# The mixer's projection: who makes the low halves of the weights

## The chip, the cores and the metric

The kernel runs on one core of a Trainium2 chip. The core has a matrix engine (TensorE, "PE" in the profile, with "PEld" for its weight loads), VectorE ("DVE"), ScalarE ("ACT"), GpSimd ("POOL") and SyncE ("SP"), which issues most of the DMAs. Each engine works through its own queue of instructions in order; between engines there are semaphores. The metric is the device time of one execution in microseconds (us); the median of three runs is used.

## The reference

One layer of a streaming encoder on a sequence of 1024 rows of width 1024, all in float32:

```python
h = sublayer(h, 0, swiglu_1, 0.5)          # feed-forward block, 1024 -> 2816 -> 1024
h = sublayer(h, 1, token_mixer, 1.0)       # the mixer
h = sublayer(h, 2, swiglu_2, 0.5)          # feed-forward block

def token_mixer(u, w_in, ...):
    proj = u @ w_in                        # 1024 x 5120
    qa, ka, va, qd, kd, vd, ga, gd = jnp.split(proj, IN_SPLITS, axis=-1)
    ya = stick_breaking_attention(heads(qa, 8), heads(ka, 8), heads(va, 8))
    yd = differential_attention(qd1, qd2, kd1, kd2, heads(vd, 4), lam)
    yd = rms_norm(yd, subln) * (1.0 - lambda_init)
    merged = jax.nn.sigmoid(ga) * (ya @ w_branch_sb) + jax.nn.sigmoid(gd) * (yd @ w_branch_da)
    return merged @ w_out
```

Each sublayer has a normalisation and a modulation before it and a normalisation and a gate behind it. The mixer's first product is the projection `proj = u @ w_in`; its columns are the queries, keys and values of two kinds of attention and the two gates.

## The kernel before, in words

**Products in two halves.** TensorE multiplies a rounded form of float32 ("fp32r"). To keep the precision, each operand is cut in a high half (the value rounded) and a low half (the value less its high half), and a product is made of three matmuls: high by high, high by low, low by high. For a weight tile the helper `split` (lines 135 to 143) does this: SyncE loads 128 x 1024 numbers into a tile `raw` (line 138, two buffers), ScalarE casts it to `wsH` (line 141), and VectorE subtracts, `wsL = raw - wsH` (line 142). `wsH` and `wsL` have four buffers each. `split` takes the engine of the subtraction as an argument, VectorE by default.

**The mixer.** Its first part projects and attends, its second merges. In the first part the projection is cut in jobs (class `Job`, line 791). A job owns one or two weight tiles and makes one slice of the projection: `QJob` and `KJob` 128 columns of queries or keys (eight jobs each, one weight tile each), `GateJob` 128 columns of a gate (sixteen, one tile), `VJob` 256 columns of values (four, two tiles). That is 8 + 8 + 16 + 4 x 2 = 40 weight tiles. A job of 128 columns runs 48 matmuls of 512 columns (lines 813, 815, 817), the third of which is the first to read `wsL`.

**Attention, and what fills it.** Eight units follow one another, four of stick-breaking attention (two heads each) and four of differential attention. In a unit, TensorE makes scores (lines 938, 939), ScalarE and VectorE turn them into weights, TensorE transposes them (lines 955, 956), ScalarE and VectorE cut the transposed weights in halves (`tH`, line 960, 963 or 965; `tL`, line 961, 964 or 966), and TensorE multiplies them with the values (line 1021 or 1066). In the stick-breaking units VectorE's part is a scan (line 1010) and a product of two tiles (line 1011) for each row block; in the differential units a scaling (line 1055) and a combination (line 1056). The matmuls of the jobs for the next unit and of the gates are put between those of the attention by `fill` and `advance`: in each call the next few matmuls of the first job in the list are traced, and `advance_` (line 923) calls `load` for the first two jobs of the list, so that a job's tiles are asked for one job ahead.

**What sets the order.** The instructions of each engine are put in order when the program is built, by the Tile framework's planner: it starts from the order in which they are traced and lets each engine take what its own model of times says is ready. Where a buffer is used again, it adds the waits. So an instruction that goes to another engine can also change the order of those around it. GpSimd's queue holds little in the mixer: `KJob` (lines 866, 867) has it copy each half of the keys to the other 64 partitions, 64 instructions of 64 x 512. SyncE's queue holds, in the mixer, the loads of `raw`, the stores of the gates (line 878) and the stores of the attention's results (lines 1027, 1088).

**The first jobs.** The first `QJob`, `KJob` and `VJob` have their tiles loaded while the last product of the first feed-forward block still runs. The second part of the mixer (the merge) calls `split` directly, for `wbs`, `wbd` and `wo`, 32 tiles; the two feed-forward blocks have helpers of their own for their weights (line 226).

Of the kernel before, what the change touches and what calls it, by code (L numbers as in the profile page):

```python
# [770 lines left out]
def mixer(e):  # L771
# [5 lines left out]
    V, ACT, PE, POOL, SP = nc.vector, nc.scalar, nc.tensor, nc.gpsimd, nc.sync  # L777
    split, mm3, wproj, ident = n.split, n.mm3, n.wproj, n.ident
# [7 lines left out]
    with tc.tile_pool(name="mixa", bufs=1, side="left", reuse_waits="tile") as pa, \  # L786
# [4 lines left out]
        class Job:  # L791
# [7 lines left out]

            def load(self):  # L800
                if self.w is None:
                    self.w = [split(s) for s in self.srcs]

            def step(self):
                if self.it is None:
# [342 lines left out]
        for u in range(8):  # L1148
            sb = u < 4
            if u == 4:  # L1150

                with tc.issue_after(last_act[0].ins):
                    load = ACT.add_instruction(mybir.InstLoadActFuncSet(
                        name=nc.get_next_instruction_name(), engine=ACT.engine, act_func_set_id=EXP_LN_TABLE))
                order.enter_context(tc.issue_after(load.ins if hasattr(load, "ins") else load))
# [196 lines left out]
```

## Time and profile before

| | us |
|---|---|
| median of three runs (lowest, highest) | 2268.05 (2264.48, 2269.99) |
| the profiled execution's own time | 2263.8 |
| its span in the profile | 2261.9 |
| granted TensorE clock, mean | 0.988 |
| PE busy | 2169.0 (96%) |
| DVE busy | 1565.4 (69%) |
| ACT busy | 1043.2 (46%) |
| POOL busy | 70.2 (3%) |

How to read the profile: an engine is busy while it executes; a row of a group of instructions gives line, engine, operation, what is written and read, the shape and the count, then busy time and the mean of one in ns, then the idle time of that engine just before them and what ended it. A table by stretches gives the busy time of each engine in a piece of the span, with the number of its instructions in brackets. A timeline has the start, the duration and the instruction, and in square brackets the idle time before it.

### The profile page before, as it was taken

Reading aid. Unit: us, or ns where it says so; the run is one execution under the profiler, and the core shown is the slowest. Engines: PE = TensorE matmul, PEld = TensorE weight load, DVE = VectorE, ACT = ScalarE, POOL = GpSimd, SP = SyncE. Lnnn points to the kernel's source line nnn. Section 1 sums busy time; section 2 is a strip of 40 time slices with the busy share of each in tenths; the row PEclk is TensorE's granted clock in tenths of the full one; section 3 lists DMA queues with packets and bytes.
Section 4 is the critical chain, followed back from the end, with each engine's and each line's share of the span. In section 5 each row is a group of like instructions: output and inputs, shape, how many; then the busy total and the mean of one; then the engine's idle time right before and its main releaser. Section 6 shows DMA issues by size and latency. Waiting matters only on the chain. (4 is left out here: it accounts for less than half of the span.)

```text
span 2261.9 us, 28622 instructions
## 1 busy us (share of the span) xinstructions
PE 2169.0 (96%) x10420; PEld 1792.0 (79%) x10420; DVE 1565.4 (69%) x2612; ACT 1043.2 (46%) x1882; POOL 70.2 (3%) x90
## 2 busy tenths in 40 slices
PE   5999999999999999999999999999999999999998
PEld 3777778878887877878888988788878788887886
DVE  6886877567677687576677577656886666755566
ACT  4633323325466556455545455555743232434454
POOL 1000000000000010011011010000000000000000
PEclk8899999999999999999999999999999999999999
DMA  7284874449787111110211122764475553538676
GB/s 307 79 280 164 300 258 170 147 161 314 250 276 228 60 32 45 38 48 30 62 57 59 45 96 75 236 200 139 149 242 186 177 177 135 186 117 270 210 225 217
DMA packets 137677, 364.38 MB, mean 161 GB/s; under 512 B 16704, under 2 KB 20800, under 8 KB 137536
## 3 DMA queue, kind: packets, MB, share of 16 engines
q1 hardware_dynamic: 135904, 356.79, 46.6%
q0 software_dynamic: 1632, 5.77, 0.7%
q8 instruction: 81, 1.33, 0.2%
q14 instruction: 60, 0.49, 0.1%
HBM read 272.32 MB, written 90.18 MB: 160 GB/s over the span
## 5 line engine op out<-in xcount | busy, mean ns | idle before, releaser
L813 PE MATMUL pps<-uH,wsH 128*128 128x512 f32 x512 | 209.0, 408 | 0.0
L815 PE MATMUL pps<-uL,wsH 128*128 128x512 f32 x512 | 204.5, 399 | 0.0
L817 PE MATMUL pps<-uH,wsL 128*128 128x512 f32 x512 | 203.6, 398 | 0.0
L226 DVE TENSOR_TENSOR tbL<-stg,tbH 128x512 fp32r<-128x512 f32 x154 | 105.9, 690 | 104.8 <-ACT tbH L225 104.3
L225 ACT CAST tbH<-stg 128x512 fp32r<-128x512 f32 x154 | 95.7, 621 | 156.7 <-DMA stg<-d_T 113.1
L298 PE MATMUL bank<-uH,wsH 128*128 128x512 f32 x352 | 142.2, 406 | 6.4 <-DVE uH L180 2.9
L584 PE MATMUL bankA<-tbL,sbH 128*128 128x512 f32 x352 | 138.8, 394 | 6.3 <-DVE tbL L226 6.3
L299 PE MATMUL bank<-uL,wsH 128*128 128x512 f32 x352 | 140.2, 398 | 1.4 <-POOL uL L181 1.3
L300 PE MATMUL bank<-uH,wsL 128*128 128x512 f32 x352 | 138.7, 395 | 0.0
L583 PE MATMUL bankA<-tbH,sbH 128*128 128x512 f32 x352 | 138.4, 395 | 0.1
L585 PE MATMUL bankA<-tbH,sbL 128*128 128x512 f32 x352 | 138.3, 393 | 0.1
L142 DVE TENSOR_TENSOR wsL<-raw,wsH 128x1024 fp32r<-128x1024 f32 x72 | 88.0, 1222 | 69.3 <-ACT wsH L141 68.0
L226 DVE TENSOR_TENSOR sbL<-stg,sbH 128x512 fp32r<-128x512 f32 (+1 forms) x176 | 108.2, 620 | 29.6 <-ACT sbH L225 26.9
L225 ACT CAST wsH<-s 128x1024 fp32r<-128x1024 f32 x88 | 92.0, 1049 | 72.4 <-DVE s L332 54.2
L225 ACT CAST sbH<-stg 128x512 fp32r<-128x512 f32 (+1 forms) x176 | 98.2, 565 | 52.7 <-DMA stg<-hd_A 37.6
L365 ACT COPY q<-bank 128x512 f32<-128x512 f32 x44 | 25.8, 586 | 207.1 <-PE bank L300 207.1
L817 PEld LDWEIGHTS pps<-uH,wsL 128*128 128x128 f32 x512 | 96.8, 189 | 17.4
L226 DVE TENSOR_TENSOR wsL<-s,wsH 128x1024 fp32r<-128x1024 f32 x88 | 107.2, 1219 | 3.5 <-ACT wsH L225 3.5
L813 PEld LDWEIGHTS pps<-uH,wsH 128*128 128x128 f32 x512 | 97.6, 191 | 14.3
L815 PEld LDWEIGHTS pps<-uL,wsH 128*128 128x128 f32 x512 | 97.1, 190 | 14.2
L225 ACT CAST wsH<-raw 128x1024 fp32r<-128x1024 f32 (+1 forms) x88 | 73.2, 834 | 71.5 <-PE bank L299 38.9
L583 PE MATMUL bankB<-tbH,sbH 128*128 128x512 f32 x264 | 102.8, 389 | 0.0
(247 smaller groups left out, 5941.2 us busy)
## 6 DMA issues: line engine op xcount, KB each, us to landing
wada<-in_wada SPq DMA_DIRECT2D x56, 512.0 KB, 5.2
raw<-in_wg SPq DMA_DIRECT2D x50, 512.0 KB, 6.4
raw<-in_wu SPq DMA_DIRECT2D x50, 512.0 KB, 4.5
raw<-in_wd SPq DMA_DIRECT2D x44, 512.0 KB, 4.5
stg<-hd_A SPq DMA_DIRECT2D x88, 256.0 KB, 4.2
stg<-d_S SPq DMA_DIRECT2D x88, 256.0 KB, 3.5
stg<-d_T SPq DMA_DIRECT2D x88, 256.0 KB, 3.8
d_S<-s SPq DMA_DIRECT2D x40, 512.0 KB, 2.7
```

Of the source, the lines that this page charges most:

```text
L142: eng.tensor_sub(l, raw, h.bitcast(F32))
L225: ACT.copy(h, src)
L226: V.tensor_sub(l, src, h.bitcast(F32))
L298: PE.matmul(ps, H[:, ks], bH, start=first and k == 0, stop=False, skip_group_check=not first)
L299: PE.matmul(ps, H[:, ks], bL, start=False, stop=False, skip_group_check=not first)
L300: PE.matmul(ps, L[:, ks], bH, start=False, stop=k == 3, skip_group_check=not first)
L583: PE.matmul(ps, sH[:, ts], tH, start=first, stop=False, skip_group_check=not check)
L584: PE.matmul(ps, sH[:, ts], tL, start=False, stop=False, skip_group_check=not check)
L585: PE.matmul(ps, sL[:, ts], tH, start=False, stop=last, skip_group_check=not check)
L813: PE.matmul(ps, aH, bH, start=i == 0, stop=False)
L815: PE.matmul(ps, aH, bL, start=False, stop=False)
L817: PE.matmul(ps, aL, bH, start=False, stop=i == n - 1)
```

## The change

`Job.load` hands GpSimd to `split`, which uses it for the subtraction. Load, cast and buffers stay as they are, and so do the 32 tiles of the merge, which call `split` without the argument.

```diff
             def load(self):
                 if self.w is None:
-                    self.w = [split(s) for s in self.srcs]
+                    self.w = [split(s, eng=POOL) for s in self.srcs]
```

The helper that is called, unchanged:

```python
    def split(src, pool=None, tag="ws", bufs=4, eng=V):
        raw = wpool.tile([P, D], F32, name="raw", tag="raw", bufs=2)
        SP.dma_start(raw, src)
        h = (pool or wpool).tile([P, D], F32R, name="wsH", tag=tag + "H", bufs=bufs)
        l = (pool or wpool).tile([P, D], F32R, name="wsL", tag=tag + "L", bufs=bufs)
        ACT.copy(h, raw)
        eng.tensor_sub(l, raw, h.bitcast(F32))
        return h, l
```

## The prediction

> **What bounds the kernel now.** I first read the page's busy times, then a table by stretches over the mixer's projection and attention, cut at the change of units: the run-in (644 to 780 us), the four stick-breaking units (780 to 1100) and the four differential units (1100 to 1420).
>
> ```profile
> PE 2169.0 (96%) x10420; PEld 1792.0 (79%) x10420; DVE 1565.4 (69%) x2612; ACT 1043.2 (46%) x1882; POOL 70.2 (3%) x90
> ...
> core 0: us, PE busy (x) PEld busy (x) DVE busy (x) ACT busy (x) POOL busy (x), PEclk, DMA share, GB/s
> 644.00:780.00 136.00, 128.87 (x681) 110.33 (x680) 92.84 (x166) 76.72 (x148) 5.33 (x8) 0.97 0.56 182
> 780.00:1100.00 320.00, 299.48 (x1708) 249.16 (x1707) 232.37 (x322) 177.88 (x399) 29.28 (x32) 0.99 0.13 40
> 1100.00:1420.00 320.00, 317.90 (x1798) 275.45 (x1797) 224.17 (x677) 158.27 (x345) 18.09 (x24) 1.00 0.21 70
> ```
>
> TensorE bounds the whole and each of these stages. Its idle time is all that a change on another engine can win: 136 - 128.87 = 7.1 us in the run-in, 320 - 299.48 = 20.5 us in the stick-breaking units, 320 - 317.90 = 2.1 us in the differential units; 29.7 us in all. The rest of its time is matmuls, whose number stays. So the question is what the 20.5 us wait for. From the waits of TensorE between 780 and 1100 (us in total, times, longest):
>
> ```profile
> PE pav L1021 <- DVE tL L961: 10.8, 7, 3.0
> PE pav L1021 <- ACT tH L965: 3.0, 4, 1.9
> PE trp L956 <- DVE be L1011: 2.1, 3, 1.1
> PE pav L1021 <- DVE tL L966: 1.9, 5, 0.7
> ```
>
> VectorE ends 10.8 + 2.1 + 1.9 = 14.8 us of these waits, each time with work of the attention. Nobody in the mixer's first part waits for the low halves themselves: in the view of line 142 the only waiters are the merge's matmuls (L201).
>
> ```profile
> L142 DVE TENSOR_TENSOR wsL<-raw,wsH x72: 1204/1224/1227, 644.5 to 1571.5; 128x1024 fp32r<-128x1024 f32 x72
> ...
> who waited for it (us, times):
>   PEld ops L201: 0.6, 1
>   PE ops L201: 0.2, 1
> ```
>
> The attention's waits on VectorE look like this (timeline, 802 to 808.5):
>
> ```profile
> 802.41 2.28 DVE L1010 TENSOR_TENSOR_SCAN f<-f 128x1024 f32<-128x1024 f32 x1
> ...
> 803.00 1.05 ACT L141 CAST wsH<-raw 128x1024 fp32r<-128x1024 f32 x1
> ...
> 804.61 0.67 DVE L961 TENSOR_TENSOR tL<-trp,tH 128x512 fp32r<-128x512 f32 x1
> 805.19 1.21 DVE L1011 TENSOR_TENSOR be<-be,f 128x1023 f32<-128x1023 f32 x1
> ...
> 805.33 0.51 PE L1021 MATMUL pav<-tL,v 128*128 128x256 f32 x2 [1.67 <-DVE tL L961]
> ...
> 806.65 1.22 DVE L142 TENSOR_TENSOR wsL<-raw,wsH 128x1024 fp32r<-128x1024 f32 x1
> ...
> 807.79 0.28 DVE L966 TENSOR_TENSOR tL<-trp,tH 128x128 fp32r<-128x128 f32 x1
> ...
> 808.13 0.33 PE L1021 MATMUL pav<-tL,v 128*128 128x128 f32 x1 [0.32 <-DVE tL L966]
> ```
>
> The large gap, 1.67 us, comes from a long scan ahead of `tL`, with no weight work in it; only the small one, 0.32 us, stands behind a `wsL`.
>
> **The change part by part.** *What it takes off VectorE.* Forty subtractions of 1224 ns (the row above; 72 less the merge's 32), 49.0 us. Also the time in which VectorE stands at the head of its queue waiting for the cast. In the stick-breaking units:
>
> ```profile
> L1010 DVE TENSOR_TENSOR_SCAN f<-f 128x128 f32<-128x128 f32 (+3 forms) x64 | 86.8, 1362 | 15.6 <-ACT f L1007 15.1
> L1011 DVE TENSOR_TENSOR be<-be,f 128x127 f32<-128x127 f32 (+3 forms) x64 | 48.1, 757 | 1.1
> ...
> L142 DVE TENSOR_TENSOR wsL<-raw,wsH 128x1024 fp32r<-128x1024 f32 x15 | 18.3, 1223 | 9.1 <-ACT wsH L141 8.1 <-PE trp L956 1.0
> ```
>
> That is 18.3 + 9.1 = 27.4 us given back to VectorE in the stage that has the gaps.
>
> *What it adds on GpSimd.* No row shows this subtraction there. The nearest is the same operation at half the width, at the start of the kernel, and what stood beside it on VectorE:
>
> ```profile
> L181 POOL TENSOR_TENSOR uL<-u,uH x6: 1278/1572/1713, 23.0 to 54.4; 128x512 fp32r<-128x512 f32 x6
> ...
> 20.52 1.23 DVE L226 TENSOR_TENSOR wsL<-raw,wsH 128x1024 fp32r<-128x1024 f32 x1
> ...
> 23.00 1.28 POOL L181 TENSOR_TENSOR uL<-u,uH 128x512 fp32r<-128x512 f32 x1 [21.69 <-DVE uH L180]
> ...
> 23.42 1.94 DVE L226 TENSOR_TENSOR wsL<-raw,wsH 128x1024 fp32r<-128x1024 f32 x1 [0.51 <-ACT wsH L225]
> ```
>
> Twice the width costs no less than 1.28 us and no more than 2 x 1.71 = 3.4 us; I take 2 x 1.28 = 2.5 us (an estimate), as 1.28 us is the undisturbed one of the six. Forty are 100 us, on an engine that is busy 5 + 29 + 18 = 53 us of these 776.
>
> The section on elementwise work in the Trainium skill's GPSIMD Engine Reference gives 4497 ns against 2293 ns for an addition of 2048 columns; by that ratio of 1.96 it would be 2.4 us here, which would change the sums below by a twenty-fifth.
>
> *What the two engines do to each other.* The second quoted VectorE row took 1.94 us where the first took 1.23: GpSimd's subtraction had started at 23.00 and ended at 24.28, and VectorE's, begun at 23.42, ran most of its own length after that. It goes the other way round too (timeline, 1052 to 1059, against the view of the key copies):
>
> ```profile
> L866 POOL CAST kd<-kd x32: 608/612/2413, 741.1 to 1314.8; 64x512 fp32r<-64x512 f32 x32
> ...
> 1053.14 2.29 DVE L1010 TENSOR_TENSOR_SCAN f<-f 128x1024 f32<-128x1024 f32 x1
> 1053.42 2.41 POOL L866 CAST kd<-kd 64x512 fp32r<-64x512 f32 x1 [5.26 <-ACT kd L864]
> 1055.34 0.66 DVE L865 TENSOR_TENSOR kl<-pps,kd 64x512 fp32r<-64x512 f32 x1
> ```
>
> A copy of 0.61 us takes 2.41 us beside a scan. So operations of VectorE with both inputs in SBUF (scans, lines 1011, 142, 226) and GpSimd's take turns, whole instruction by whole instruction. In the stick-breaking units scans and products hold 86.8 + 48.1 = 134.9 of 320 us, 42%. Fifteen subtractions hold 15 x 2.5 = 37.5 us, of which VectorE would want 42%: 15.8 us blocked. Net, VectorE gains 27.4 - 15.8 = 11.6 us on 232.4 us of work, 5.0%. The gaps that it causes, 14.8 us, shrink with it by 0.7 us if they follow its load, and I round this to 1.0 us, for the queue is also freer of waits. From below: a gain of all that VectorE causes, 14.8 us, excluded in practice by the scans in the gaps; from above: 15 holds that each push a chain, priced among the rivals.
>
> The Trainium skill's SBUF — State Buffer says, in its section on the engine side, that VectorE and GpSimd share one pair of ports as an exclusive lock, and that the loser "fully blocks". The trace agrees (1.94 for 1.23, 2.41 for 0.61). Without that rule the sum would give VectorE all 27.4 us, 12% of its load, and a gain of 1.7 us; with it, 0.7.
>
> *The differential units and the run-in.* TensorE is idle for 2.1 us in the first, so there is nothing to win, and what blocks VectorE (lines 1055, 1056) is hidden by a TensorE that has job matmuls to run. In the run-in four subtractions move beside the last feed-forward product, whose 7.1 us of idle TensorE come later, from normalisation. Both 0; cover gone, one gap of a hold, 2.5 us, for each.
>
> *The weights themselves.* They come 1.3 us later, or up to 2.3 us more if a scan holds the lock. TensorE reads most of them tens of us later; the tightest is the first tile of the differential units:
>
> ```profile
> 1099.31 1.22 DVE L142 TENSOR_TENSOR wsL<-raw,wsH 128x1024 fp32r<-128x1024 f32 x1
> ...
> 1102.00 0.60 PE L817 MATMUL pps<-uH,wsL 128*128 128x512 f32 x1
> ```
>
> Begun at 1099.31, it would end at 1101.8 with 2.5 us: 0.2 us in hand. Taken as 0; 3.4 us would cost 0.7.
>
> *The queues.* GpSimd now waits for casts, and the key copies stand behind that; SyncE's loads into `raw` wait for the subtraction of two tiles before, and stores stand behind them.
>
> ```profile
> SPq L138 <- DVE wsL L142: 140.4, 26, 23.2
> ...
> ACT wsH L141 <- DMA raw<-in_win: 3.8, 2, 2.5
> ...
> PEld z L938 <- POOL kl L867: 0.5, 1, 0.5
> ```
>
> SyncE is parked at these loads for 140.4 us already, yet the cast waited for one only twice, 3.8 us: a load freed 1.3 us later is still early. TensorE waited for a key copy once, 0.5 us. Both 0; with the cover gone, one hold of 2.5 us for a copy at the edge of a unit.
>
> *The sum.* The profiled execution took 2263.8 us (2261.9 of span and 1.9 around it); less 1.0 is 2262.8. That execution is 4.25 us below the median of the runs, 2268.05, so the median forecast is 2267 us. A measurement of this kernel tells 0.3%, 6.8 us, from no change.
>
> **The rivals.** *A, faster: the gaps follow VectorE's queue more than its load.* What counts would be how soon `tL` gets a turn, and the planner, with VectorE freer, would put it ahead of scans. Then two thirds of the 14.8 us go: 2268 - 9.9 = 2258 us. For it: 8.1 us of VectorE's standing at the cast; against it: the 1.67 us gap has no `wsL` near it. Chance 0.25.
>
> *B, slower: the lock falls into the scan chains.* In the timeline above the cast ends at 804.05, while the scan runs to 804.69. GpSimd then takes the lock at 804.69 and holds it to 807.19; the product due at 805.19 starts 2.0 us later, and `tL` of line 966 comes, with 1.22 us of `wsL` gone from the queue, 0.8 us later than now; that wait ends last for TensorE. Were that so for all 15, 12 us: 2280 us. It decides from the point at which casts end during a scan more often than between chains; scans alone hold 86.8 of 320 us, 27%, which speaks against it, and for it speaks that the gaps stand just at the long scans, where nothing is in hand. Chance 0.15.
>
> The Trainium skill's Perfetto Trace Analysis, in its section on optimizing, warns that offloading between these two engines "might not help" for their shared port; that is B's mechanism or my forecast, by its size.
>
> *C, slower: lateness on GpSimd reaches TensorE.* Key copies behind a blocked subtraction and the tight tiles: two holds at the starts of units and 3.4 us at the tight tile, 2 x 2.5 + 3.4 = 8.4 us, 2276 us. For it: one queue now carries both; against it: the slack above. Chance 0.10.
>
> **How the numbers follow.** The forecast has 0.50, with its own range of 2261 to 2275 (6.8 us on either side). Faster by over 0.3% is A, 0.25; slower B and C, 0.25. The range takes in A's and B's points with a little of the runs' scatter (2264.48 to 2269.99 before): 2256 to 2282.
>
> **What would show it.** Line 142 should have 32 instructions on VectorE and 40 on GpSimd, of about 2.5 us, longer beside scans; products of line 1011 longer than now by the blocked time, about 16 us in all; VectorE's busy time between 780 and 1100 (which counts the blocked time) near 232 - 18 + 16 = 230 us; TensorE's idle time there near 20 us. TensorE waiting for a `wsL` or a key copy would mean C; longer waits for `tL`, B; idle time near 10 us, A. Wrong altogether would be a TensorE that gains or loses more than 7 us outside the mixer.

## The result

| | before | after |
|---|---|---|
| median of five runs (lowest, highest), us | 2268.05 (2264.48, 2269.99) | 2283.43 (2277.98, 2288.25) |
| profiled execution, its span, us | 2263.8, 2261.9 | 2282.8, 2281.0 |

The change makes the kernel slower: the ratio of the times is 1.0073, with a 95% interval of 1.0057 to 1.0089. The median lies 1.4 us above the upper end of the predicted range.

The first part of the page after, and the views of the moved line and of its neighbours on VectorE. In a view of a line, the three numbers are the shortest, the median and the longest in ns; in a group's row they are the busy time in us and the mean in ns.

```profile
PE 2176.9 (95%) x10420; PEld 1797.9 (79%) x10420; DVE 1555.0 (68%) x2572; ACT 1044.6 (46%) x1882; POOL 164.9 (7%) x130
```

```profile
L142 POOL TENSOR_TENSOR wsL<-raw,wsH 128x1024 fp32r<-128x1024 f32 x40 | 98.4, 2464 | 555.1 <-ACT wsH L141 492.6 <-issue 43.6 <-PE z L939 12.7
```

```profile
L142 POOL TENSOR_TENSOR wsL<-raw,wsH x40: 2362/2402/3345, 644.0 to 1361.7; 128x1024 fp32r<-128x1024 f32 x40
L142 DVE TENSOR_TENSOR wsL<-raw,wsH x32: 1210/1224/1228, 1388.6 to 1588.5; 128x1024 fp32r<-128x1024 f32 x32
```

```profile
L1010 DVE TENSOR_TENSOR_SCAN f<-f 128x128 f32<-128x128 f32 (+3 forms) x64 | 90.5, 1416 | 20.0 <-ACT f L1007 19.5
L1011 DVE TENSOR_TENSOR be<-be,f 128x127 f32<-128x127 f32 (+3 forms) x64 | 58.0, 908 | 1.2
```

```profile
L1011 DVE TENSOR_TENSOR be<-be,f x64: 277/816/2842, 786.7 to 1110.1; 128x127 f32<-128x127 f32 x8, 128x255 f32<-128x255 f32 x8, 128x383 f32<-128x383 f32 x8, 128x511 f32<-128x511 f32 x8
```

Forty subtractions moved and take 2.40 us each on GpSimd in the median; the products of line 1011, which nobody edited, take 58.0 us in place of 48.1, the longest of them 2.84 us; the scans of line 1010 take 90.5 in place of 86.8. Where the time went is read from stages that end at the same work. I cut both executions at the start of the first, the third, the 21st and the last of the 32 jobs of 128 columns. Before, then after:

```profile
727.80:780.20 52.40, 50.22 (x324) 46.25 (x323) 29.05 (x53) 23.84 (x44) 5.33 (x8) 0.97 0.18 61
780.20:1188.20 408.00, 387.45 (x2230) 327.19 (x2229) 290.11 (x489) 218.10 (x486) 34.99 (x40) 0.99 0.15 46
1188.20:1401.20 213.00, 211.40 (x1180) 181.60 (x1179) 155.37 (x492) 106.96 (x240) 12.38 (x16) 1.00 0.20 67
```

```profile
730.90:781.90 51.00, 48.82 (x324) 44.72 (x323) 26.07 (x50) 23.73 (x44) 9.79 (x11) 1.00 0.20 64
781.90:1203.90 422.00, 390.68 (x2229) 328.79 (x2228) 284.02 (x466) 218.25 (x485) 90.55 (x63) 0.98 0.14 44
1203.90:1418.50 214.60, 211.65 (x1179) 181.85 (x1179) 152.08 (x481) 107.43 (x240) 37.47 (x27) 1.00 0.20 67
```

(The columns are the stretch, its length and the busy time of PE, PEld, DVE, ACT and POOL, then the granted clock.) The middle row, which holds the stick-breaking units and the first differential one, has 14.0 of the 19.1 us by which the spans differ. In it TensorE's idle time went from 408.00 - 387.45 = 20.6 us to 422.00 - 390.68 = 31.3 us, while VectorE was busy for 6 us less. So 10.7 us of the row's 14.0 are idle time, and 3.2 us are longer matmuls; of the rest, 1.7 us lie ahead of the row (781.9 - 780.2) and 1.6 and 1.8 us behind it.

TensorE's waits between 780 and 1112 after the change:

```profile
PE pav L1021 <- DVE tL L961: 10.8, 7, 3.0
PE pav L1021 <- ACT tH L965: 5.3, 6, 1.9
PE pav L1021 <- DVE tL L966: 4.0, 5, 2.1
PE trp L956 <- DVE be L1011: 3.5, 4, 1.4
PE trp L955 <- DVE be L1011: 1.3, 1, 1.3
```

The waits that stood there before (`tL` of line 961 behind a scan) are the same 10.8 us in seven. New are those behind line 1011: 3.5 + 1.3 us in place of 2.1, and `tH` of line 965 and `tL` of line 966, which follow it, 9.3 us in place of 4.9. One such place, the same one that the prediction showed for before:

```profile
805.38 2.28 DVE L1010 TENSOR_TENSOR_SCAN f<-f 128x1024 f32<-128x1024 f32 x1
...
806.02 1.05 ACT L141 CAST wsH<-raw 128x1024 fp32r<-128x1024 f32 x1
...
807.14 2.69 POOL L142 TENSOR_TENSOR wsL<-raw,wsH 128x1024 fp32r<-128x1024 f32 x1 [20.73 <-ACT wsH L141]
...
807.58 0.66 DVE L961 TENSOR_TENSOR tL<-trp,tH 128x512 fp32r<-128x512 f32 x1
808.16 2.75 DVE L1011 TENSOR_TENSOR be<-be,f 128x1023 f32<-128x1023 f32 x1
...
810.84 0.41 DVE L964 TENSOR_TENSOR tL<-trp,tH 128x256 fp32r<-128x256 f32 x1
...
811.60 0.33 PE L1021 MATMUL pav<-tH,v 128*128 128x128 f32 x1 [1.53 <-ACT tH L965]
```

GpSimd's subtraction comes in at the end of the scan. The product behind it, 1.21 us before, takes 2.75 us. The `tL` of line 961 between them, one of whose inputs (`trp`) lies in PSUM, keeps its 0.66 us. The `tL` behind the product is late, then `tH`, and TensorE stands for 1.53 us; before, this second gap was 0.32 us. Five of the 64 products stand beside a subtraction of GpSimd in this trace, and each of the five takes 2.74 to 2.84 us.

### The profile page after: what moved, and what is told of

Its sections match the earlier page's. It is cut to its first block, busy times and chain, and to the rows that moved or that the text cites. A ratio compares the mean times of both kernels' runs of the same rounds, so it can differ in the third digit from the quotient of the medians.

```text
span 2281.0 us, 28648 instructions
## 1 busy us (share of the span) xinstructions
PE 2176.9 (95%) x10420; PEld 1797.9 (79%) x10420; DVE 1555.0 (68%) x2572; ACT 1044.6 (46%) x1882; POOL 164.9 (7%) x130
## 4 chain that ended last, share of the span: by engine, by line
PE 59%; DVE 21%; DMA 10%; ACT 5%; issue 3%; SPq 0%; DVEq 0%; ACTq 0%
PE bank L300 8%; PE bank L298 8%; PE bank L299 8%; PE pps L815 4%; PE pps L813 4%; PE pps L817 4%; DMA stg<-d_T 3%; DVE f L1010 3%; DMA stg<-in_wd 2%; DVE wsL L226 2%; PE bankA L583 2%; PE bankA L584 2%; PE bankA L585 2%; DMA wada<-in_wada 1%; DVE be L1011 1%
## 5 line engine op out<-in xcount | busy, mean ns | idle before, releaser
L142 POOL TENSOR_TENSOR wsL<-raw,wsH 128x1024 fp32r<-128x1024 f32 x40 | 98.4, 2464 | 555.1 <-ACT wsH L141 492.6
L1010 DVE TENSOR_TENSOR_SCAN f<-f 128x128 f32<-128x128 f32 (+3 forms) x64 | 90.5, 1416 | 20.0 <-ACT f L1007 19.5
```

The source lines that it names most:

```text
L1010: V.tensor_tensor_scan(fr, fr, fr, 1.0, ALU.mult, ALU.bypass)
```

## The experiments

The theory is the one of the prediction's rival B: VectorE's instructions with two inputs in SBUF and GpSimd's that read SBUF take turns, so each subtraction on GpSimd holds up VectorE's scans and products, and these set the pace of the attention. The rivals are lateness of the weights or of the queues (C), a new order of the instructions from the planner, and, on the other side, that time given back to VectorE has a worth (the forecast and A).

### The same reading, with nothing moved

`split` gets a flag that `Job.load` sets for the 36 tiles that are loaded within the units:

```diff
         eng.tensor_sub(l, raw, h.bitcast(F32))
+        if beside:
+            x = mpool.tile([P, D + 64], BF16, name="scr", tag="junk", bufs=1)
+            POOL.tensor_sub(x[:, :D], raw, h.bitcast(F32))
```

> VectorE keeps all its subtractions (as in the kernel before); beside that GpSimd makes the same difference of raw and wsH once more for the 36 tiles that are loaded within the units, into a scratch tile that nobody reads. Theory (turns at SBUF): GpSimd's 36 holds of about 2.4 us block VectorE's scans and products as in the changed kernel, and nothing is given back: slower than before by at least as much as the change, 15 to 30 us; VectorE's line 1011 rows as long as after the change. Rival (lateness of the weights or of the queues, or the new order of the instructions): nobody waits for this work, so within 5 us of the kernel before.

Measured: 2301.59 us, ratio 1.0141 (1.0109 to 1.0173), about twice the loss of the change. The spare work in this kernel, and what it does to VectorE's own subtractions and to the products (line numbers are shifted by the edit):

```profile
L145 POOL TENSOR_TENSOR scr<-raw,wsH 128x1024 bf16<-128x1024 f32 x36 | 111.3, 3092 | 397.5 <-ACT wsH L141 303.1 <-issue 93.9
```

```profile
L142 DVE TENSOR_TENSOR wsL<-raw,wsH 128x1024 fp32r<-128x1024 f32 x43 | 66.9, 1556 | 30.9 <-ACT wsH L141 30.7
L1015 DVE TENSOR_TENSOR be<-be,f 128x127 f32<-128x127 f32 (+3 forms) x64 | 57.4, 901 | 1.1
```

No engine takes a result from this work, and no weight comes from GpSimd. The products are as long as after the change (57.4 and 58.0 us). By the ratio the loss is 32 us, just above the 15 to 30 of the expectation: the spare subtractions are longer than the moved ones (3092 ns in the mean against 2464), and VectorE's own subtractions, which now stand beside them, take 1556 ns in place of 1224.

Lateness of the weights or of the queues can make little of this loss: in the mixer's first part of this trace TensorE's weight loads wait for a low half once, 0.8 us, and for a key copy once, 2.3 us (0.5 before), and ScalarE's casts wait for `raw` for 5.6 us in all, against 6.2 before. The planner's order can make none of it: in the traces of this kernel and of the kernel before, the instructions of TensorE, VectorE and ScalarE stand in the same order throughout, by operation, tiles and shape.

### The same place and time on GpSimd, with nothing read

```diff
+        if beside:
+            x = mpool.tile([P, D + 64], BF16, name="scr", tag="junk", bufs=1)
+            ACT.copy(x[:, :1], h[:, :1].bitcast(F32))
+            for _ in range(3):
+                POOL.memset(x[:, :D], 0.0)
```

> As the run with GpSimd's spare subtraction, but GpSimd fills the scratch tile with a constant three times instead, behind a one-column copy by ScalarE that ties it to the same place in time; it reads nothing from SBUF. Theory (turns only between instructions that read): VectorE's rows of line 1011 keep their length of before (748 ns median), and the time stays within 5 us of before. If any GpSimd work in these places costs time: 10 us or more slower, as with the subtraction.

Measured: 2271.71 us, ratio 1.0016 (1.0007 to 1.0026).

```profile
L1017 DVE TENSOR_TENSOR be<-be,f 128x127 f32<-128x127 f32 (+3 forms) x64 | 48.3, 760 | 1.1
```

```profile
L147 POOL MEMSET scr<- 128x1024 bf16 x108 | 103.6, 959 | 359.7 <-ACT scr L145 355.8
```

GpSimd is as busy with it as with the moved subtractions after the change (103.6 us against 98.4), in the same places, and the products are as short as before, though 13 of the 64 have a filling beside them. So it is the reading, not GpSimd's being busy. This agrees with the Trainium skill's SBUF — State Buffer, section "Who interferes with whom": an instruction of VectorE with two SBUF inputs contends with one of GpSimd that reads SBUF, and not with one that only writes it. A loss of 3.6 us (1.6 to 5.9, by the ratio) is left, which is clear of zero; 36 small copies of ScalarE are among its possible causes, and it was not taken apart.

### VectorE freed, and nobody loaded

`split` is handed the low half of the first tile, `low`, and leaves its subtraction out once that has been made:

```diff
-        eng.tensor_sub(l, raw, h.bitcast(F32))
+        if low is None or not lows:
+            eng.tensor_sub(l, raw, h.bitcast(F32))
...
-                    self.w = [split(s) for s in self.srcs]
+                    self.w = []
+                    for s in self.srcs:
+                        if low:
+                            self.w.append((split(s, low=low[0])[0], low[0]))
...
```

> Leaves out 39 of the 40 subtractions: all jobs of the projection use the low half of the first tile. So VectorE is freed as by the change and nobody takes the work on. Theory: the gaps come from the scans and the time given back to VectorE is worth little: 0 to 5 us faster than before. Rival A of the prediction (the gaps follow VectorE's queue): 8 to 12 us faster.

Measured: 2268.42 us, ratio 0.9992 (0.9980 to 1.0003): no difference that is clear of zero. The middle stage of this kernel, by the same cuts:

```profile
779.60:1184.20 404.60, 384.47 (x2229) 325.39 (x2229) 265.83 (x466) 218.31 (x485) 33.06 (x40) 1.00 0.15 46
```

VectorE has 290.11 - 265.83 = 24.3 us less to do in it, and TensorE's idle time is 404.60 - 384.47 = 20.1 us, against 20.6 before. In the traces, then, the time given back is worth half a microsecond; by the interval of the times it is worth 4.5 us at most. So rival A's 9.9 us are excluded. The forecast's 1 us is too small for these times to tell, and a version that only takes these subtractions off VectorE has hardly anything to win.

This kernel also settles the new order of the instructions. Apart from the subtractions of weights, its trace has the order of the changed kernel, not of the one before: against the changed kernel 2 of VectorE's other 2364 instructions stand elsewhere, 1 of ScalarE's 1882 and 3 of TensorE's 10420; against the kernel before, 106, 29 and 40 do. With the changed order and nothing on GpSimd, nothing is lost.

### Shorter turns

`split` makes the low half in several pieces on GpSimd, for all 40 tiles:

```diff
-        eng.tensor_sub(l, raw, h.bitcast(F32))
+        for i in range(cuts):
+            c = slice(i * D // cuts, (i + 1) * D // cuts)
+            eng.tensor_sub(l[:, c], raw[:, c], h[:, c].bitcast(F32))
```

> GpSimd makes the low halves as in the change, but each in four subtractions of 256 columns. Theory (turns, whole instruction by whole instruction): a hold is 0.6 to 0.7 us in place of 2.4, VectorE gets its turn after one of them, so the loss falls from 15 us to 0 to 7. Rival (lateness of the weights, GpSimd's queue): GpSimd's work is as long or longer, so the loss stays at 12 us or more.

> As the run with four cuts, with eight subtractions of 128 columns for each tile. Theory (turns): VectorE's waits get shorter still, but each piece has a fixed part and there are twice as many turns: 2 to 7 us slower than before, like four cuts; never faster than before, since freeing VectorE altogether won nothing.

Measured: four pieces 2275.52 us, ratio 1.0025 (1.0009 to 1.0040); eight pieces 2277.46 us, ratio 1.0045 (1.0028 to 1.0063), against 1.0073 with whole tiles. GpSimd's work and the products with four pieces:

```profile
L144 POOL TENSOR_TENSOR wsL<-raw,wsH 128x256 fp32r<-128x256 f32 x160 | 129.6, 843 | 526.0 <-ACT wsH L141 465.5 <-issue 42.9 <-PE z L941 12.4
```

```profile
L144 POOL TENSOR_TENSOR wsL<-raw,wsH x160: 723/744/2191, 645.3 to 1356.0; 128x256 fp32r<-128x256 f32 x160
```

```profile
L1013 DVE TENSOR_TENSOR be<-be,f x64: 280/826/1516, 787.7 to 1104.8; 128x127 f32<-128x127 f32 x8, 128x255 f32<-128x255 f32 x8, 128x383 f32<-128x383 f32 x8, 128x511 f32<-128x511 f32 x8
```

GpSimd works longer (129.6 us against 98.4, a piece 744 ns in the median) and the loss falls to about a third, 5.7 us (2.0 to 9.1): the longest product is 1.52 us in place of 2.84, and the longest before the change was 1.54. VectorE's turn comes after one piece. The order is again that of the changed kernel, with VectorE's and ScalarE's instructions all in the same places. This is what turns of whole instructions give, and what lateness or order does not. Eight pieces lose 10 us (6.4 to 14.3), more than the 2 to 7 expected, though the intervals of four and eight overlap; the reason was not found.

### Which tiles

`Job.load` picks the engine by the unit in which the tile is loaded, for example:

```diff
-                    self.w = [split(s) for s in self.srcs]
+                    self.w = [split(s, eng=POOL if 0 <= unit[0] < 4 else V) for s in self.srcs]
```

> GpSimd makes the low halves of the 16 tiles that are loaded in the four stick-breaking units, VectorE those of the other 24. Theory (holds between scans and products): nearly the whole loss is here, 8 to 14 us slower than before. If the loss went by the number of tiles that GpSimd makes: 16 of 40, 6 us.

> GpSimd makes the low halves of the 20 tiles that are loaded in the four differential units, VectorE those of the other 20. Theory: TensorE had 2 us of idle time there and its queue has other matmuls, so 1 to 4 us slower than before. By the number of tiles: half of the loss, 8 us.

> GpSimd makes the low halves of the first four tiles alone, beside the last product of the first feed-forward block. Theory: no scans there, 0 to 2 us slower than before. If the longer half-clock stretch behind the first feed-forward block (10.2 us after the change, 3.4 before, from about 688) belongs to the change: 3 us.

> GpSimd makes the low halves of the tiles that are loaded in the first differential unit alone (the first six or so of the 20), VectorE all others. In the trace of the run with all four differential units, the first two of these holds fall into the last product of the last stick-breaking unit (2.76 us in place of 1.21), and TensorE's idle time grows there. If that place is most of the loss: 3 to 6 us slower than before. If the loss goes by the number of tiles: 2 to 3 us.

> GpSimd makes the low halves of the tiles that are loaded in the last three differential units alone. If nearly all of the loss of the differential units sits at their start: 0 to 2 us slower than before. If small operations that wait out a hold (line 1045, 2.36 us at most in place of 0.15) cost TensorE time too: 3 to 6 us.

| tiles on GpSimd | median, us | ratio (95%) | by the ratio, us |
|---|---|---|---|
| 16, stick-breaking units | 2277.71 | 1.0039 (1.0026 to 1.0053) | 8.8 (5.9 to 12.0) |
| 20, differential units | 2275.57 | 1.0033 (1.0019 to 1.0048) | 7.5 (4.3 to 10.9) |
| 4, run-in | 2269.86 | 1.0010 (0.9998 to 1.0022) | 2.3 (-0.5 to 5.0) |
| first differential unit alone | 2269.40 | 1.0007 (0.9995 to 1.0019) | 1.6 (-1.1 to 4.3) |
| last three differential units alone | 2271.56 | 1.0013 (1.0000 to 1.0026) | 2.9 (0.0 to 5.9) |

The last column is the ratio less one, times 2268. The first three rows give 18.6 us together, and the change as a whole 16.6 (12.9 to 20.2): the parts add up. A tile of the stick-breaking units costs 0.55 us, one of the differential units 0.38; that of the run-in is not clear of zero. So the stick-breaking units carry about half of the loss, not nearly all of it, and the expectation for the differential units was too low. By the last two rows their loss is 4.5 us, which lies within the interval of the row of all four; 4 to 8 us is as close as these times come. The middle row of the kernel with the stick-breaking units moved, then the middle and the last row of the one with the differential units moved, by the same cuts:

```profile
780.50:1196.70 416.20, 387.59 (x2229) 326.76 (x2229) 286.59 (x475) 218.28 (x486) 67.66 (x54) 0.99 0.14 45
```

```profile
784.10:1195.80 411.70, 388.98 (x2229) 327.84 (x2228) 285.07 (x480) 218.09 (x485) 57.64 (x49) 0.98 0.15 45
1195.80:1410.40 214.60, 211.64 (x1180) 181.79 (x1179) 152.17 (x481) 107.41 (x239) 37.48 (x27) 1.00 0.20 67
```

With the stick-breaking units' tiles moved, TensorE's idle time in the middle row is 28.6 us against 20.6 before. With the differential units' it is 22.7, and 3.0 against 1.6 in the last row: 3.5 us more, at the lower end of what the times allow.

What the trace shows of it is two things. At the seam, the first two subtractions run back to back, and the last product of the last stick-breaking unit stands beside them (timeline of the run with the differential units):

```profile
1100.82 5.67 POOL L142 TENSOR_TENSOR wsL<-raw,wsH 128x1024 fp32r<-128x1024 f32 x2 [38.13 <-issue]
...
1101.49 2.76 DVE L1012 TENSOR_TENSOR be<-be,f 128x1023 f32<-128x1023 f32 x1
...
1104.31 0.47 PE L957 MATMUL trp<-ident,be 128*128 128x128 f32 x1 [1.03 <-DVE be L1012]
```

And within the units small operations wait out a hold. The maximum of two numbers per row, before and after the change:

```profile
L1045 DVE TENSOR_TENSOR mx<-mx x32: 136/152/161, 1151.6 to 1388.3; 128x1 f32<-128x1 f32 x32
```

```profile
L1045 DVE TENSOR_TENSOR mx<-mx x32: 139/154/2358, 1166.4 to 1405.7; 128x1 f32<-128x1 f32 x32
```

```profile
1345.62 2.63 POOL L142 TENSOR_TENSOR wsL<-raw,wsH 128x1024 fp32r<-128x1024 f32 x1 [11.29 <-ACT wsH L141]
1345.91 2.36 DVE L1045 TENSOR_TENSOR mx<-mx 128x1 f32<-128x1 f32 x1
```

Four of the 32 are lengthened so, each beside a subtraction of GpSimd. Whether they cost TensorE time was not shown.

The loss of the run-in is not clear of zero, so the question that its expectation put about the slower clock stays open. The granted clock behind the first feed-forward block (0.91, 0.74 and 0.68), before the change, after it, and with the run-in's tiles alone moved:

```profile
680.00:700.00 20.00, 15.05 (x77) 11.94 (x76) 18.01 (x33) 12.85 (x27) 0.00 (x0) 0.91 0.89 292
```

```profile
680.00:700.00 20.00, 14.21 (x62) 11.30 (x61) 16.54 (x31) 11.63 (x27) 0.00 (x0) 0.74 0.84 283
```

```profile
680.00:700.00 20.00, 13.17 (x49) 10.31 (x48) 16.75 (x31) 11.07 (x24) 0.00 (x0) 0.68 0.83 277
```

The kernels that give GpSimd no subtraction of these four tiles have 0.83 to 0.97 in this row, the four that do 0.68 to 0.83. So a slower clock tends to go with the change, but one trace of each kernel does not show what it costs.

## Why the prediction was wrong

**What bounds the kernel** was right: TensorE bounds these stages, and the loss is its idle time, read where the prediction looked for it.

**The price of the moved instruction** was right: 2.40 us against an estimate of 2.5, and 1.96 times VectorE's 1.224 us, which is the ratio that the Trainium skill's GPSIMD Engine Reference gives in its section on elementwise work.

**That the engines take turns** was right, and so, nearly, was the amount. I expected 15.8 us blocked in the stick-breaking units; the products of line 1011 grew by 58.0 - 48.1 = 9.9 us and the scans by 90.5 - 86.8 = 3.7 us, 13.6 us together. The prediction put all of it into the products, and spread it over all subtractions; it came from the few that met a scan or a product.

**The step that failed** is the one from VectorE's load to TensorE's wait: "The gaps that it causes, 14.8 us, shrink with it by 0.7 us if they follow its load". By this step the 27.4 us freed are worth 27.4 / 232.4 x 14.8 = 1.7 us to TensorE, and the 15.8 us blocked cost it 15.8 / 232.4 x 14.8 = 1.0 us. The freed part is indeed worth little: VectorE was idle for over a quarter of the stage anyway, and 24.3 us taken off it changed TensorE's idle time by 0.5 us in the kernel without low halves. The blocked part was priced at about a ninth of its cost. The kernel that moves the stick-breaking units' tiles alone loses 8.8 us (5.9 to 12.0), and TensorE's idle time grows by 8.0 us in its trace. What counts is whether a hold falls into the chain of scan, product and `tL` that TensorE waits for. There most of a blocked microsecond is lost, and a freed one elsewhere is not given back in exchange. The prediction set 27.4 us freed against 15.8 us blocked as if they were of one kind. By the rows that it had, the freed part was to be priced near nothing (the 1.67 us gap with no `wsL` near it), and then the blocked part is all that is left.

**The 0 for the differential units** was the second step that failed: moving their tiles alone loses 7.5 us (4.3 to 10.9). That TensorE was idle for only 2.1 us there bounds a gain and not a loss.

**Rival B** had this mechanism, 0.8 us for each of 15 subtractions and 2280 us, with a chance of 0.15. The place that it worked out happened as it said: the product waits out the hold. It was to be 2.0 us late; it ended at 808.16 + 2.75 = 810.91, against 805.19 + 1.21 = 806.40 before, and less the 2.97 us by which the scan ahead of it starts later (805.38 - 802.41) that is 1.5 us. Its size in the stick-breaking units, 12 us, is at the top of the measured 5.9 to 12.0. That its 2280 us come near the measured 2283.43 is in part luck: it had all 15 subtractions cost 0.8 us each, where only five products were lengthened, by about 1.6 us each, and it lacked the differential units, where 4 to 8 us were lost. The range, which ended at 2282 us, had no room for these either.

**Rival A** falls with the kernel without low halves. **Rival C** has no support: in the changed kernel no matmul of the mixer's first part is shown waiting for a low half or a key copy, and the kernel with the spare subtraction loses more with all weights from VectorE. The new order of the instructions, which the prediction did not price, is excluded from both sides: the kernel with the spare subtraction keeps the old order and loses, and the kernel without low halves has the new one and does not.

**The 0 for the run-in** could not be told from -0.5 to 5.0 us. **The 0 for the queues** agrees with the trace after the change, in which TensorE does not wait for a key copy.

## What to carry to other kernels

An operation with two inputs in SBUF that goes from VectorE to GpSimd leaves its shadow on VectorE, as here: GpSimd holds the reading for the whole instruction (2.4 us here where VectorE needed 1.2), and the next scan or product waits it out. Before counting time given back, check whether the freed engine ends the waits of the bounding one with that work; if not, there is little to gain and the holds remain. A stage in which the bounding engine is hardly idle has nothing to win from such a move, but it can lose. Where such work must go to GpSimd, shorter instructions can help: pieces of a quarter cost about a third of the loss here, and pieces of an eighth no less than that.

## What the runs showed of the hardware

- Even the smallest instruction waits out a hold: a maximum of one number per row on VectorE took up to 2358 ns in place of 161 at most.
- A subtraction on VectorE with one input in PSUM and one in SBUF (`tL` of line 961) was not lengthened: 0.66 us beside GpSimd's subtraction, 0.67 in the same place before.
- GpSimd's filling of a tile, 103.6 us of it beside the same scans and products, did not lengthen them (48.3 against 48.1 us); its reading did (57.4 us).
- On GpSimd a subtraction of 256 columns took 744 ns in the median, one of 1024 columns 2402 ns.
